# One written order for all engines from the last recurrence block to the entry of the feed-forward part

## The chip, the cores and the metric

The kernel runs on one core of a Trainium2 chip. A core has five engines, each with its own queue of instructions that it works through in order: TensorE (PE, matmuls, with PEld for its weight loads), VectorE (DVE), ScalarE (ACT), GpSimd (POOL) and SyncE (SP, which here issues nearly all DMA transfers). An instruction that waits for data holds everything behind it on its own engine. The metric is the time of one execution in device microseconds, as the median of the timed runs.

## What is computed

One hybrid decoder layer over 2048 tokens of width 1024, all in float32. Cut to what matters:

```python
xn   = rms_norm(h, pre_mix_norm)
proj = xn @ w_in                                   # state-space and recurrence inputs
y_ssd  = ssd_mixer(proj[:, :1544], ...)            # 8 heads, chunks of 128 tokens, gated by silu(z), normed
y_rwkv = rwkv7_mixer(proj[:, 1544:], ...)          # 8 heads: S = S*w + (S a) b + v k, y = S r, per token
mix = concat([y_ssd, y_rwkv]) @ w_out
h   = h + rms_norm(mix, post_mix_norm)
hn  = rms_norm(h, pre_ffn_norm)
u   = causal_dwconv(hn @ ffn_w_up, ...)            # 2 x 2816 columns, 3 taps
f   = (silu(gate(u)) * val(u)) @ ffn_w_down
out = h + rms_norm(f, post_ffn_norm)
```

## The kernel before

Matmul operands are split into a high and a low fp16 part, and each product is made of three matmuls (high x high, high x low, low x high). The work has three phases.

*R* (`phase_R`) is the recurrence: 16 blocks of 128 tokens. A block makes its input products (`d`, `c`), the gram matrices (`gr`), and a triangular solve on 32x32 pieces (`solve`: 31 small steps of L754 and L760 on POOL and DVE, then a round trip through DRAM, L766 and L772, and the products `pw` and `po`, L841 and L845). The second half of a block runs beside the first half of the next.

*S* (`phase_S`) is the state-space part: 8 pairs of two chunks of 128 tokens. Per chunk it makes the gate products `z` (L1216, a PSUM bank of its own with one buffer, emptied by ACT's copy `sz`, L1222), the decay products `bc` (L1261, L1262), the outputs `py` and `pf`, the state `pst`, and then the output projection `o` (L1344, 24 matmuls of 512 columns per half) with the post norm (L1347 to L1376). Per pair the cumulative decay is turned over on PE (`acs`, L1192: the flip), split into three bf16 parts on DVE (`pp`, L1195 to L1198), written to DRAM by SP (`rows`, L1200) and read back in another layout (`R`, L1255), one R per chunk. The post norm writes H (L1360), turns the normed tokens over by transposing transfers (`tu`, L1372, L1373), joins the parts on POOL (`hT`, L1375) and writes HN (L1376), which the feed-forward part reads. Output weights are loaded by SP as `ost` (L1116) and split by ACT and others (`split_w`, L287) into `wo`. The row roots of the norms are two short POOL instructions (L302, L303).

*F* (`phase_F`) is the feed-forward part in two halves of 1024 tokens, 22 column groups f in each, with seven products (L1658) per f over sums and differences of quarter blocks. Its operands are the token parts `b` (loads `hs`, splits at L1504) and the weight parts `w` (loads `us`, sums at L1630, splits at L1499 on ACT and L1506 on DVE). Products go through `C` (L1672 on ACT, L1676 on DVE), the convolution taps (L1711) and the gate, and every fourth f the `down` products (L1894) follow.

What sets the order: PE's instructions stand in the order in which the program writes them, everywhere. Block 15 of R is written by the plan `LAST`, the rest of it beside the first state-space steps by `DRAIN` and `S_DRAIN`, the state space by `S_PLAN` and `S_TAIL` (with steps of the first two f's of F in the places marked F). DVE, ACT, POOL and SP follow a written order only in the blocks up to 14 and in what `Program.run()` plans of F (from its third f on); between, the framework's scheduler orders their instructions by its own costs and the dependencies. Some of SP's loads are tied to an earlier transfer there by `pace` (L291), which adds an ordering with no semaphore. In F, `Program.add` (L69) plans a step when `prog.on` is set, and before that runs it at once:

```python
    def add(self, engine, us, fn, reads=(), writes=()):
        if not self.on:
            fn()
            return
```

## Time and profile before

| | |
|---|---|
| median of 3 timed runs | 2552.05 us (2547.22 to 2556.14) |
| the profiled execution | 2552.89 us |
| its span, first to last instruction | 2551.1 us |
| mean granted TensorE clock | 0.980 of full speed |
| PE busy | 2406.4 us, 94% of the span |
| DVE busy | 1921.5 us, 75% |
| last block of R alone on PE | about 814 to 864 us |
| end of R beside the first state-space chunks | about 864 to 932 us |
| output projection `o` | 937 to 1314 us |
| products of F | 1273 us to the end (1273.0 is the first, in between the last `o`) |
| products of f = 4 | about 1388 to 1405 us |

The profile is of one execution. A row of the timeline or of a group names its start and length in us, the engine, the line, the operation, the tile it writes and those it reads, the shape and, with x, how many instructions of one kind stand together; a bracket behind it is the idle time of the engine just before it and what ended it. A row of the waits names the engine and line that waited, the engine and line that it waited for, and the total in us, the number of waits and the longest. SPq is SP's queue of DMA issues; there a length is the time of issuing.

### The profile page before, as it was taken

How to read it: one execution, taken by the hardware profiler on the slowest of the kernel's cores; microseconds unless marked ns; L12 is line 12 of the kernel's file. 1: busy time of each engine (PE TensorE's matmuls, PEld its weight loads, DVE VectorE, ACT ScalarE, POOL GpSimd, SP SyncE). 2: the span in 40 equal slices, each digit the busy share in tenths (PEclk: the TensorE clock that was granted, in tenths of full speed). 3: DMA queues.
4: the chain of work that ended last, by engine and by line, in shares of the span. 5: the costliest groups of instructions: out<-in, count | busy, mean ns of one | idle time of the engine just before them, and what ended most of it. 6: DMA issues, size and time to landing. Idle time of an engine off the chain costs nothing. (4 is left out here: it accounts for less than half of the span.)

```text
span 2551.1 us, 53834 instructions
## 1 busy us (share of the span) xinstructions
PE 2406.4 (94%) x21212; PEld 1520.3 (60%) x21212; DVE 1921.5 (75%) x3687; ACT 1204.6 (47%) x2407; POOL 1231.3 (48%) x1237
## 2 busy tenths in 40 slices
PE   4899999999999899999988999999979999999998
PEld 4789999999998655555533444444434444444443
DVE  6768877877787557768888799999999826455557
ACT  6555666566556444445444554444543432213132
POOL 2233444344444524446687675686847622223135
PEclk8899999999999989999999999999999999999999
DMA  7233233323322445556664544544446543333243
GB/s 220 68 71 71 56 79 78 65 58 78 85 56 61 163 128 140 145 160 179 179 201 154 181 138 161 174 143 167 140 132 223 170 121 103 101 102 104 84 160 107
DMA packets 344412, 319.12 MB, mean 125 GB/s; under 512 B 203232, under 2 KB 248672, under 8 KB 340832
## 3 DMA queue, kind: packets, MB, share of 16 engines
q1 hardware_dynamic: 342864, 314.12, 41.8%
q8 instruction: 166, 2.72, 0.5%
q10 hardware_dynamic: 1296, 1.58, 0.2%
q14 instruction: 86, 0.70, 0.1%
HBM read 187.85 MB, written 110.99 MB: 117 GB/s over the span
## 5 line engine op out<-in xcount | busy, mean ns | idle before, releaser
L1658 PE MATMUL u<-b,w 128*128 128x512 f16 x3696 | 810.1, 381 | 29.7 <-DVE C L1676 10.2
L1658 PEld LDWEIGHTS <-w 128*128 128x128 f16 x3696 | 363.0, 98 | 473.9 <-issue 37.9
L324 PE MATMUL d<-xt,wr 128*128 128x129 f16 x5376 | 333.1, 224 | 25.1 <-DMA xt<-xh 15.6
L324 PEld LDWEIGHTS <-wr 128*128 128x128 f16 x5376 | 319.0, 100 | 40.2 <-issue 21.7
L1894 PE MATMUL d<-dw,fa 128*128 128x512 f16 x1512 | 332.0, 379 | 4.7 <-DMA dw<-DW 2.4
L1894 PEld LDWEIGHTS <-fa 128*128 128x128 f16 x1596 | 156.5, 98 | 204.5 <-issue 17.0
L1676 DVE TENSOR_TENSOR C<-u,C 128x512 f32<-128x512 f32 x220 | 150.5, 685 | 156.3 <-PE u L1658 146.4
L324 PE MATMUL c<-xt,wc 128*128 128x131 f16 x3072 | 198.8, 225 | 12.0 <-ACT rc L558 6.3
L324 PEld LDWEIGHTS <-wc 128*128 128x128 f16 x3072 | 184.2, 99 | 18.9 <-issue 11.0
L1907 DVE TENSOR_TENSOR acc<-d,acc 128x512 f32<-128x512 f32 x212 | 140.2, 683 | 52.7 <-PE d L1894 51.8
L1504 POOL TENSOR_TENSOR fa<-p,fa 128x512 f16<-128x512 f32 x100 | 142.3, 1436 | 40.3 <-ACT fa L1499 40.3
L1506 DVE SCALAR_TENSOR_TENSOR w<-us,w 128x512 f16<-128x512 f32 x132 | 146.0, 1117 | 14.8 <-ACT w L1499 13.7
L1711 DVE SCALAR_TENSOR_TENSOR p<-C,fpar,p 128x1024 f32<-128x1024 f32 x88 | 128.8, 1464 | 35.4 <-ACT p L1707 35.2
L582 DVE SCALAR_TENSOR_TENSOR ca<-c,cw,ca 128x128 f32<-128x128 f32 x360 | 113.5, 344 | 25.3 <-ACT ca L572 21.4
L754 DVE TENSOR_TENSOR tmp<-atl,xl 128x60 f32<-128x60 f32 (+24 forms) x465 | 119.1, 256 | 17.4 <-DMA atl<-ATd 5.9
L1711 DVE SCALAR_TENSOR_TENSOR a<-C,fpar,a 128x1024 f32<-128x1024 f32 x88 | 125.8, 1429 | 4.4 <-ACT a L1707 3.0
L1499 ACT ACTIVATE fa<-p 128x512 f16<-128x512 f32 x110 | 65.5, 623 | 132.6 <-DVE p L1724 120.8
L1630 POOL TENSOR_TENSOR us<-us,us 128x512 f32<-128x512 f32 x66 | 106.3, 1614 | 41.4 <-DVE w L1506 22.2
L760 DVE TENSOR_TENSOR xl<-xl,tmp 128x60 f32<-128x60 f32 (+24 forms) x465 | 113.0, 243 | 14.4
L1672 ACT ACTIVATE C<-u 128x512 f32<-128x512 f32 x88 | 52.2, 593 | 145.0 <-PE u L1658 128.0
L1717 POOL COPY fcarry<-C 128x2 f32<-128x2 f32 x88 | 41.1, 468 | 163.3 <-DVE C L1676 163.3
L1499 ACT ACTIVATE w<-us 128x512 f16<-128x512 f32 x132 | 80.6, 624 | 79.1 <-POOL us L1630 44.6
(325 smaller groups left out, 4425.5 us busy)
## 6 DMA issues: line engine op xcount, KB each, us to landing
UW<-w SPq DMA_DIRECT2D x154, 256.0 KB
w<-UW SPq DMA_DIRECT2D x154, 256.0 KB
us<-in_w_u_dram SPq DMA_DIRECT2D x88, 256.0 KB
DW<-dw SPq DMA_DIRECT2D x70, 256.0 KB
dw<-DW SPq DMA_DIRECT2D x56, 256.0 KB
hs<-HN SPq DMA_DIRECT2D x48, 256.0 KB
r<-in_w_d_dram SPq DMA_DIRECT2D x10, 1024.0 KB
xin<-in_x_dram SPq DMA_DIRECT2D x16, 512.0 KB
```

The lines of the kernel that those rows point to most:

```text
L324: nc.tensor.matmul(ps, w[:, a, kt, :], xt[:, b, kt, cols], start=n == 0, stop=n == 3 * KT - 1)
L582: V.scalar_tensor_tensor(out=acc[:, q], in0=m["rc", e][:, q, k:k + 128], scalar=cw[:, e + q, k:k + 1], in1=acc[:, q], op0=ALU.mult, op1=AL ...
L754: chain.tensor_tensor(out=self.tmp[:, :k, :n], in0=self.atl[:, j, j + 1:32].unsqueeze(1).to_broadcast([P, k, n]), in1=self.xl[:, :k, j:j + ...
L760: chain.tensor_tensor(out=self.xl[:, :k, j + 1:32], in0=self.xl[:, :k, j + 1:32], in1=self.tmp[:, :k, :n], op=ALU.add)
L1499: S.activation(h, src, AF.Copy, **({} if scale is None else {"scale": scale}))
L1504: {"V": V, "G": G_}[engine].tensor_tensor(out=l, in0=src, in1=h, op=ALU.subtract)
L1506: V.scalar_tensor_tensor(out=l, in0=src, scalar=scale, in1=h, op0=ALU.mult, op1=ALU.subtract)
L1658: nc.tensor.matmul(bk[at], self.w[i][:, u, k, :], self.half.b[i][:, k, v, :], start=start and n == 0, stop=n == 11, skip_group_check=True)
L1676: op("V", .61, lambda: V.tensor_tensor(out=part(j, x), in0=bk[at], in1=part(*a), op=ALU.add), (("u", 4 * s + at), (*(c0, c1)[a[0]], a[1])) ...
L1711: V.scalar_tensor_tensor(out=o[j], in0=C[j][:, 2 - d:1026 - d], scalar=cw[:, g, 2 - d:3 - d], in1=o[j], op0=ALU.mult, op1=ALU.add)
L1894: nc.tensor.matmul(bk[s, t], pairs[m].a[i][:, u, t * P:t * P + P], pairs[m].w[n][0][:, v, :], start=new and m == 0 and u == v == 0, stop=m ...
L1907: V.tensor_tensor(out=acc[j][:, t], in0=bk[s, t], in1=acc[j][:, t], op=ALU.add)
```

## The change

The phases are cut into named steps. A method such as `Chunk.y` or `Pair.flip` now returns a list of small functions, each for one to a few instructions, and the class `Steps` calls them by name, as R's blocks did already. A step's instructions are noted while they are traced. There are two tables: `TAIL` is the order in which the steps are traced, which sets PE's memory allocation and the dependencies; `ORDER` is one order of the same steps for all five engines, from the last steps of block 13 to the 460th step of F. For each step of `ORDER`, each of its instructions is put behind the previous one of its engine by an ordering that has no semaphore ("written order"). The 460 E steps are F's set-up (8), the steps of its first two f's, and the first 140 steps (`OPENED`) of what `Program.run()` planned for the rest. From there on `HANDS`, the planned order of before, goes on unchanged.

Besides: `pace` is gone, since the table says where SP's loads stand. Eight parameter loads (cst_s, dtb, Ab, Db, sdt, gpost, gpre2 and fpar) are issued by SP, where ACT issued them. F's products made before the planner is on are four steps of three matmuls each (one per k) instead of one step of twelve. The PSUM bank of `pf`, `py` and `pY` is chosen by the chunk's parity. The instructions themselves are as before: 34368 on PE, 3689 on DVE and 1242 on POOL in both programs; ACT goes from 2306 to 2298 and SP from 1284 to 1292, which is the eight loads. The order of PE, DVE, ACT, POOL and SP is the same in both programs up to the last block of R (the first difference on PE stands at 814 us of the profiled execution) and from f = 4 of F on (1388 to 1405 us).

Three places show how the order differs. The first is the drain, on ACT. Tiles ending in _14 or _15 belong to R's blocks, sz_1 and th_1 to state-space chunk 1, wo is the output weight. Before:

```order
L986 ACTIVATE yln_14_16994<-yt_14_16989,par_194 128x128 x4
L287 ACTIVATE wo_17701<-ost0_17710,sng_16792 128x1024
L287 ACTIVATE wo_17701<-ost1_17714,sng_16792 128x1024
L1222 ACTIVATE sz_1_17023<-z_1_16980 128x512
L992 ACTIVATE yo_14_17001<-yln_14_16994 128x4x128
L1223 ACTIVATE th_1_17024<-sz_1_17023 128x512
```

The same place on ACT now:

```order
L1456 ACTIVATE wo_17702<-ost0_17711,sng_17020 128x1024
L876 ACTIVATE ct_15_6_16902<-ca_15_6_16893 128x256
L1456 ACTIVATE wo_17702<-ost1_17715,sng_17020 128x1024
L1633 ACTIVATE sz_1_17257<-z_1_17214 128x512
L1274 ACTIVATE yln_14_17228<-yt_14_17223,par_194 128x128 x4
L1543 ACTIVATE de_1_17315<-de_1_17315 128x16
L1174 ACTIVATE qs_150_17175<-pq_150_17154 64x512
L1637 ACTIVATE th_1_17259<-sz_1_17257 128x512
```

The two splits of wo have another ACT step between them and sz_1 follows them, with the affine of block 14 (yln) behind it. The loads that the splits need stand on SP. XTd and XT1 are block 15's solve on its way through DRAM. Before:

```order
L766 DMA XTd_15_16302<-xl_15_16237 256x1x32 x4
L772 DMA XT1_230<-XTd_15_16302 32x8x32 x4
L1116 DMA ost0_17710<-in_w_o_dram 128x1024
L1116 DMA ost1_17714<-in_w_o_dram 128x1024
L1200 DMA rows_0_16978<-pp_0_16972 16x384
L1255 DMA R_0_16987<-rows_0_16978 3x8x128
L1255 DMA R_1_17278<-rows_0_16978 3x8x128
```

SP at this place now:

```order
L1434 DMA ost0_17711<-in_w_o_dram 128x1024
L1489 DMA xbc_1_17074<-XC1_66 128x2048
L1434 DMA ost1_17715<-in_w_o_dram 128x1024
L1054 DMA XTd_15_16538<-xl_15_16473 256x1x32 x4
L1434 DMA ost2_17719<-in_w_o_dram 128x1024
L883 DMA XC7_72<-ca_15_4_16818 128x2x128
L1060 DMA XT1_230<-XTd_15_16538 32x8x32 x2
L1584 DMA rows_0_17212<-pp_0_17206 16x384
```

The output weight loads stand ahead of XTd_15 instead of behind XT1, and xbc_1 and a convolution output (XC7) have moved between. The second place is on SP in the state space, at pair 2 (rows_2, R_4, R_5) beside the post norm of chunk 1 (tu_10 and tu_11, its two halves). Before:

```order
L1372 DMA_TRANSPOSE tu_10_18318<-hl_1_18300 128x4x128
L1373 DMA_TRANSPOSE tu_10_18318<-xi_1_17999 128x4x128
L1140 DMA xbc_3_18395<-XC3_68 128x2048
L1376 DMA HN0_81<-hT_10_18321 128x4x128
L1372 DMA_TRANSPOSE tu_11_18326<-hl_1_18300 128x4x128
L1373 DMA_TRANSPOSE tu_11_18326<-xi_1_17999 128x4x128
L1200 DMA rows_2_18360<-pp_2_18354 16x384
L1333 DMA yr_3_18472<-YR1_74 128x8x128
L1335 DMA xi_2_18260<-in_x_dram 128x1024
L1255 DMA R_4_18362<-rows_2_18360 3x8x128
L1255 DMA R_5_18622<-rows_2_18360 3x8x128
```

SP at this place now:

```order
L1878 DMA H1_84<-m_1_18027 128x1024
L1867 DMA_TRANSPOSE tu_10_18319<-xi_1_18000 128x4x128
L1584 DMA rows_2_18361<-pp_2_18355 16x384
L1686 DMA R_4_18363<-rows_2_18361 3x8x128
L1819 DMA yr_3_18473<-YR1_74 128x8x128
L1867 DMA_TRANSPOSE tu_11_18327<-xi_1_18000 128x4x128
L1867 DMA_TRANSPOSE tu_11_18327<-hl_1_18301 128x4x128
L1822 DMA xi_2_18261<-in_x_dram 128x1024
L1489 DMA xbc_3_18396<-XC3_68 128x2048
L1887 DMA HN0_81<-hT_10_18322 128x4x128
L1887 DMA HN0_81<-hT_11_18330 128x4x128
L1686 DMA R_5_18623<-rows_2_18361 3x8x128
```

rows_2 and R_4 stand ahead of the second half's transposes, and R_5 stands behind both HN writes of chunk 1. The third place is on DVE at the end of the state space, chunk 14's output yt_14 beside the first weight parts of F. Before:

```order
L1296 TENSOR_TENSOR yt_14_20776<-py_14_20917,yt_14_20776 128x512
L1297 TENSOR_TENSOR yt_14_20776<-yt_14_20776,sz_14_20830 128x512
L1305 TENSOR_SCALAR yt_14_20776<-yt_14_20776,sgr_20933 128x256 x2
L1317 TENSOR_TENSOR ST1_16803<-pst_14_20954,ST1_16803 128x512
L1235 TENSOR_TENSOR Xdt_15_20971<-px_15_20975,dtt_7_20462 128x512
L1239 TENSOR_TENSOR yt_15_20981<-px_15_20975,Db_16788 128x512
```

DVE at this place now:

```order
L1779 TENSOR_TENSOR yt_14_20774<-py_14_20918,yt_14_20774 128x512
L1796 TENSOR_TENSOR ST1_17026<-pst_14_20955,ST1_17026 128x512
L1780 TENSOR_TENSOR yt_14_20774<-yt_14_20774,sz_14_20831 128x512
L1654 TENSOR_TENSOR Xdt_15_20977<-px_15_20972,dtt_7_20479 128x512
L1978 SCALAR_TENSOR_TENSOR w4_0_0_21524<-us_0_001_21502,w4_0_0_21524 128x512
L1742 TENSOR_TENSOR of_15_20994<-pf_15_20991,E_7_20669 128x512
L1660 TENSOR_TENSOR yt_15_20979<-px_15_20972,Db_17019 128x512
L1976 TENSOR_TENSOR b2_0_21429<-hs00010_21416,b2_0_21429 128x512
L1978 SCALAR_TENSOR_TENSOR w1_0_0_21512<-us_0_000_21498,w1_0_0_21512 128x512
L1768 TENSOR_SCALAR yt_14_20774<-yt_14_20774,sgr_20935 128x256
```

The scaling by sgr stood right behind the product with sz; now the state, the next chunk's first steps and token and weight parts of F stand between.

The diff, cut to its core (a line or two of each table):

```diff
+class Steps:
+    made, kind = None, ""
+    def do(self, name, *a, only=None):
+        key = (name, *a)
+        if key not in self.todo:
+            self.todo[key] = getattr(self, name)(*a)
+        steps = self.todo[key]
+        for i in range(len(steps)) if only is None else (only,):
+            step, steps[i] = steps[i], None
+            if step:
+                note(".".join(str(v) for v in (f"{self.kind}{self.number()}", *key)) + f"/{i}", step)
...
-S_PLAN = """
-c.begin Z c.off c.decay.0 Z p.norm Z Z c.decay.1 p.o.0.0 p.o.0.1 c.keys t.sums q.post.0 s.steps q.post.1 c.y t.flip
-n.rows p.o.1.0 c.state p.o.1.1
-"""
...
+TAIL = """
+R14.solve R13.state.1 R13.finish.0 R14.d.13 R14.conv.7 R14.transposed.0 R13.values R14.conv.5 R15.load
...
+OPENED = 140
+ORDER = """
+R14.conv.7/9 R13.state.1/3 R15.d.0/0 R13.state.1/4 R14.conv.7/10 R13.state.1/6 R13.finish.0/0 R14.d.13/1 R15.d.1/0
...
-        def load_x(self):
-            self.xt = wk.tile([P, 2, KT, TB], F16, name="xs" + self.sf, tag="xt", bufs=2)
-            pace(tc, K, nc.sync.dma_start(self.xt, XN[self.b]), "atl")
+        def load(self, what):
+            def rows():
+                if what == 0:
+                    self.xt = wk.tile([P, 2, KT, TB], F16, name="xs" + self.sf, tag="xt", bufs=2)
+                    nc.sync.dma_start(self.xt, XN[self.b])
...
-        S.dma_start(fp, K.par_dram[:, NCOLS - NP_F:NCOLS])
+            early, mid, lambda: nc.sync.dma_start(K.fp, K.par_dram[:, NCOLS - NP_F:NCOLS]),
...
-                    def make():
+                    def make(some=range(4)):
...
+                    if not prog.on:
+                        for k in range(4):
+                            op("T", .65, lambda k=k: make((k,)))
+                        return
...
-        with tc.manual_schedule(engines={getattr(mybir.EngineType, x) for x in ("DVE", "Activation", "Pool", "SP")}):
-            prog.run()
+        todo = prog.run()
+        yield prog.entry + todo[:OPENED]
+        prog.on = None
+        with tc.manual_schedule(engines=HANDS):
+            for step in todo[OPENED:]:
+                step()
...
+    def behind(ins):
+        if ins.engine in last:
+            tc.add_manual_dep(ins, last[ins.engine].name, dep, reason="written order")
+        last[ins.engine] = ins
+
+    for step in ORDER.split():
+        for ins in made.get(step, ()):
+            behind(ins)
```

More of the change, by code (lines that the diff above doesn't have):

```diff
@@ new lines @@
+R15.merge.1 R15.update.0 C0.keys R15.state.0 C3.z.1 R15.own.1 C1.rows C0.y R15.update.1 C3.z.2 R15.state.1 R15.gate
+R15.finish.0 C0.state C3.z.3 R15.finish.1 rend E.0 X.right X.wo.0 X.wo.1 X.wo.2 X.wo.3 X.wo.4 X.wo.5 X.wo.6 X.wo.7
+P2.load.0 C1.begin C4.z.0 C1.off C1.decay.0 C4.z.1 C0.norm C4.z.2 C1.decay.1 C0.load.0 C0.load.1 C0.o.0.0 C0.o.0.1
+C1.keys P1.sums C1.y P1.flip C2.rows C0.o.1.0 C1.state C0.o.1.1 P2.load.1 C2.begin C4.z.3 C2.off C2.decay.0 C5.z.0
+C1.norm C5.z.1 C2.decay.1 C1.load.0 C1.load.1 C1.o.0.0 C1.o.0.1 C2.keys C0.post.0 P2.steps C0.post.1 C2.y C3.rows
@@ L256 @@
+E.378 E.424 C15.post.1/5 E.391 E.431 E.450 E.456 E.459 E.441 E.453 E.452 E.420 E.428 E.440 E.417 E.442 E.439 E.437
+E.446 E.458 E.457 E.448 E.449
 """
+HANDS = {getattr(mybir.EngineType, x) for x in ("DVE", "Activation", "Pool", "SP")}
 def load_consts(tc, K, pool, cst, par, rows, rows16):
@@ L1259, in decay @@
             hs, c, q = slice(4 * g, 4 * g + 4), self.c, self.q
-            bc = bank(f"bc{self.cf}{g}", "bc")
-            nc.tensor.matmul(bc, identb, mnegb, start=True, stop=False)
-            nc.tensor.matmul(bc, ones3, self.R[:, hs], start=False, stop=True)
-            for h in range(4):
-                S.activation(self.Dt[:, 4 * g + h], bc[:, h], AF.Exp, bias=q.nac[:, c, 4 * g + h:4 * g + h + 1])
-            V.tensor_tensor(
-                out=self.Dt[:, hs], in0=self.psc[:, g, :].unsqueeze(1).to_broadcast([P, 4, P]), in1=self.Dt[:, hs],
-                op=ALU.mult)
@@ L1268, in decay, with products @@
-            V.tensor_tensor(out=self.dec[:, hs], in0=bc[:, :, P - 1], in1=q.nac[:, c, hs], op=ALU.add)
-            S.activation(self.aend[:, hs], bc[:, :, P - 1], AF.Exp)
-            if g == 1:
-                S.activation(self.dec, self.dec, AF.Exp)
+            m = {}
+            def products():
+                m["bc"] = bank(f"bc{self.cf}{g}", "bc")
+                nc.tensor.matmul(m["bc"], X.identb, X.mnegb, start=True, stop=False)
+                nc.tensor.matmul(m["bc"], X.ones3, self.R[:, hs], start=False, stop=True)
@@ new lines, in y, with rows, products, square @@
+        def y(self):
+            def rows():
+                return self.yt.rearrange("p h s -> p (h s)")
+            def products():
+                py = self.py = bank_y("py" + self.cf, self.n).rearrange("p a b -> p (a b)")
+                for h in range(8):
+                    nc.tensor.matmul(
+                        py[:, 64 * h:64 * h + 64], self.Dt[:, h, :], self.Xdt[:, h, :], start=True, stop=True)
+            def square(g):
+                if g == 0:
+                    self.gs = wk.tile([P, 2], F32, name="sgs" + self.cf, tag="sgs")
+                    self.jk = wk.tile([P, 1024], BF16, name="sq" + self.cf, tag="sq")
@@ L2107, in hybrid_layer @@
-        next(F)
-        for _ in S:
-            next(F)
+        cp = ExitStack()
+        const = cp.enter_context(tc.tile_pool(name="const", bufs=1, side="left"))
+        tables = [io[n] for n in ("cst", "par", "rows", "rows16")]
+        K.hand = ExitStack()
+        blocks, front, rest = phase_R(
+            tc, K, const, tables, io["x"], io["w_r"], io["w_c"], io["wl"], io["g2"], XN, XC, YR)
+        pairs, chunks, setup = phase_S(tc, K, io["x"], io["w_z"], io["w_dt"], io["w_o"], XN, XC, YR, Hd, HN)
@@ new lines, in hybrid_layer @@
+        F = phase_F(tc, K, io["w_u"], io["w_d"], Hd, HN, out)
+        entry = next(F)
+        K.hand.close()
+    last = {ins.engine: ins for ins in traced(tc)}
+    Steps.made = {"tc": tc}
+    for step in TAIL.split():
+        step, _, part = step.partition("/")
+        name, *a = step.split(".")
+        if name == "front":
+            front()
+        elif name == "rend":
+            rest.close()
+        elif name == "const":
+            cp.close()
+        elif name == "E":
+            note(step, entry[int(a[0])])
+        elif name == "X":
+            setup.do(a[0], *(int(v) for v in a[1:]), only=int(part) if part else None)
+        else:
+            some = {"R": blocks, "P": pairs, "C": chunks}[name[0]]
+            some[int(name[1:])].do(a[0], *(int(v) for v in a[1:]), only=int(part) if part else None)
@@ L2111, in hybrid_layer @@
             pass
+    first = {}
+    for ins in traced(tc)[n:]:
+        if first.setdefault(ins.engine, ins) is ins:
+            behind(ins)
 def host_layout(inputs):
```

1082 lines of the change are left out of this document (701 added, 381 removed).

## The prediction

> **What bounds the kernel now.** I read the page first: the busy rows, then the span in 40 slices, to see whether one engine sets the time and where it doesn't.
>
> ```profile
> PE 2406.4 (94%) x21212; PEld 1520.3 (60%) x21212; DVE 1921.5 (75%) x3687; ACT 1204.6 (47%) x2407; POOL 1231.3 (48%) x1237
> PE   4899999999999899999988999999979999999998
> PEclk8899999999999989999999999999999999999999
> ```
>
> TensorE (PE) is busy 94% of the span. Each slice is 64 us. PE's digit drops below 9 at the start, at 829 to 893 us (the 14th slice), at 1276 to 1403 us, at 1850 to 1913 us and at the end; the clock's drops at 893 to 957 us. Elsewhere PE is the bound, and no order of the other engines can help there. The change leaves every order alone up to block 15 of the recurrence and from the fifth feed-forward step (f = 4) on, which the trace puts at 814 and 1405 us. So I cut the trace there, and inside by phase: the last block, its drain beside the first state-space chunks, the state-space phase, and its end with the entry of the feed-forward part.
>
> ```profile
> core 0: us, PE busy (x) PEld busy (x) DVE busy (x) ACT busy (x) POOL busy (x), PEclk, DMA share, GB/s
> 814.00:864.00 50.00, 44.95 (x745) 41.28 (x743) 31.56 (x79) 26.98 (x61) 29.18 (x50) 1.00 0.48 162
> 864.00:932.00 68.00, 54.23 (x477) 34.46 (x475) 39.76 (x98) 32.15 (x66) 26.73 (x48) 0.85 0.43 133
> 932.00:1200.00 268.00, 253.78 (x1492) 144.02 (x1490) 193.44 (x364) 121.12 (x337) 128.66 (x134) 1.00 0.53 147
> 1200.00:1405.00 205.00, 179.37 (x814) 84.42 (x815) 168.77 (x186) 98.52 (x193) 149.32 (x129) 0.93 0.58 178
> ```
>
> Length less PE busy is PE's idle time: 5.0, 13.8, 14.2 and 25.6 us, 58.6 us in all. Besides, the granted clock was 0.85 in the second stretch and 0.93 in the fourth, a loss of up to 0.15 x 68 = 10.2 and 0.07 x 205 = 14.4 us, part of it inside the gaps. Gaps and clock together are all that a new order can win, some 70 to 80 us; the matmuls stay. The waits say who holds PE (total, times, longest):
>
> ```profile
> PE bc L1262 <- DMA R<-rows: 8.7, 5, 2.4
> PE z L1216 <- ACT sz L1222: 8.4, 4, 7.7
> PE u L1658 <- DVE C L1676: 6.7, 2, 4.5
> PE u L1658 <- DVE b L1504: 6.2, 2, 4.6
> PE u L1658 <- ACT w L1499: 4.3, 1, 4.3
> PE bc L1261 <- ACT aend L1269: 3.6, 3, 2.0
> ```
>
> Six rows hold 37.9 of the 58.6 us: a DMA chain in the state-space phase, one long stall in the drain, and DVE and ACT in the entry of the feed-forward part.
>
> **The change, part by part.** It removes and adds nothing on PE; 8 parameter loads go from ACT's queue to SP's; the rest is order. I take the four stretches in turn.
>
> *814 to 864, last block.* PE's 5.0 us there are many short waits on links of chains that the new order spaces out. No row of before shows the new spacing: between nothing and all 5.0, I take half, 2.5.
>
> *864 to 932, drain.* These rows are ACT, PE, SP and the wait of SP ahead of them:
>
> ```profile
> 877.74 1.51 ACT L986 ACTIVATE yln<-yt,par 128x128 f32<-128x128 f32 x4 [1.33 <-PE yt L983]
> 887.20 2.42 ACT L287 ACTIVATE wo<-ost,sng 128x1024 f16<-128x1024 f32 x2 [7.96 <-DMA ost<-in_w_o_dram]
> 889.53 0.58 ACT L1222 ACTIVATE sz<-z 128x512 f32<-128x512 f32 x1
> 890.16 2.72 PE L1216 MATMUL z<-ws,xs 128*128 128x512 f16 x6 [7.70 <-ACT sz L1222]
> 883.48 0.92 SPq L1116 DMA_DIRECT2D ost<-in_w_o_dram  x2
> SPq L766 <- DVE xl L760: 20.9, 1, 20.9
> ```
>
> The z bank has one buffer, so PE's next z waits for ACT's sz copy (0.58 us). ACT works in order, and ahead of sz stand two splits of the output weights, whose loads SP issued only at 883.48, because it stood 20.9 us on the write of block 15's triangular solve. In the new order two of these loads are issued ahead of that write, so ACT finds its data there: the 7.7 us go. What is late next is the solve itself:
>
> ```profile
> L825 DVE STREAM_TRANSPOSE XW<-XT x2: 425/430/436, 883.3 to 884.5; 32x256 f32<-32x256 f32 x2
> L841 PE MATMUL pw<-XW,G x32: 191/191/212, 900.0 to 900.5; 32*32 32x32 f32 x32
> ```
>
> XW is ready at 884.9 and PE got to it at 900.0, a cover of 15 us, of which the 7.7 us take half. That leaves 7 us for the other gaps before it, so I don't take all of the remaining 6.1 us but half, 3. Of the clock loss of 10.2 us, which begins in this stall, I take 6. Together 7.7 + 3 + 6 = 17 us. If the solve's chain comes 8 us later in the new order, only 7 are won; with every gap and the full clock it would be 24. I stay above the middle, since the cover is a row of the trace and only its use is guessed.
>
> *932 to 1200, state space.* One of the five waits on R, with its chain:
>
> ```profile
> 989.10 0.28 PE L1192 MATMUL acs<-ident_s,nac 128*16 128x128 f32 x1
> 991.04 1.23 DVE L1198 TENSOR_TENSOR pp<-rr,pp 16x128 bf16<-16x128 f32 x1
> 994.38 1.21 SPq L1373 DMA_TRANSPOSE tu<-xi  x1
> 995.71 0.50 SPq L1200 DMA_DIRECT2D rows<-pp  x1
> 997.61 0.62 SPq L1255 DMA_DIRECT2D R<-rows  x2
> 1001.07 0.37 PE L1262 MATMUL bc<-R,ones 3*128 3x512 bf16 x1 [2.39 <-DMA R<-rows]
> ```
>
> From the flip's end (989.38) to R in place (1001.07) it takes 11.7 us. In it the rows' write is issued 3.4 us after pp is complete (992.27 to 995.71), because SP first issues two transposing transfers of the post norm. The new order puts the rows ahead of the second half's transposes, and R right behind. Without the 3.4 us the chain takes 8.3. PE's own work between flip and R was 11.7 - 2.4 = 9.3 us; in the new order it is about 7 us in this pair (24 o, 2 pb, 8 py and one bc, by the durations below) and 8 to 17 in the others. So this pair still waits some 1.1 us, others less. I leave 3.0 of the 8.7 us, the rest of 5.7 goes. Of the other 14.2 - 8.7 = 5.5 us, all short links, I take 2.3, in all 8. Bounds: 14.2 if all goes, and -6 if the rows or R come as late again as they now are early (7 pairs x 0.9 us of it uncovered).
>
> The short waits have a second cost, which these rows show:
>
> ```profile
> 1258.32 0.38 PE L1261 MATMUL bc<-mnegb,identb 128*128 128x512 bf16 x1 [1.96 <-ACT aend L1269]
> 1258.94 4.45 PE L1344 MATMUL o<-wo,yr 128*128 128x512 f16 x12
> 1263.23 2.75 PE L1344 MATMUL o<-wo,Y 128*128 128x512 f16 x12
> 1265.82 0.38 PE L1249 MATMUL pb<-ident_s,xbc 128*128 128x128 f32 x2
> 1266.04 1.23 PE L1294 MATMUL py<-Xdt,Dt 128*128 128x64 f32 x10
> ```
>
> Right behind a wait of 1.96 us twelve o products take 4.45 us, where the next twelve take 2.75: 1.7 us of clock lost to a short gap. I count these only inside the clock terms. The Trainium skill (TensorE: Matmul & The Clock Gate, Part 1) has the clock halve after an idle window of about 3.4 us or more. By that rule only the waits of 7.7, 4.6, 4.5 and 4.3 us would cost clock, and some 2 us of my sum would fall away; the trace differs, with its 1.96 us.
>
> *1200 to 1405, end of state space and entry of the feed-forward part.* PE waits for DVE and ACT here, and DVE is busy 168.8 of 205 us. What DVE itself waited for in this stretch:
>
> ```profile
> DVE w L1506 <- ACT w L1499: 7.9, 5, 2.9
> DVE xi L1364 <- POOL pnr L303: 7.3, 5, 2.7
> DVE m L1358 <- POOL por L303: 4.2, 4, 2.1
> DVE yt L1305 <- POOL sgr L303: 4.2, 3, 2.1
> ```
>
> DVE's 36.2 us of idle time are what the end of this stretch can come forward by. In the new order the scaling of yt has six other instructions between itself and its operand's last step instead of none, so sgr's 4.2 us go; the post norm's two waits (11.5) and ACT's splits (7.9) are spaced out less, and I take half, 9.7. That makes 13.9. Against it stands 2 us for DVE work that is stretched when POOL's share rises: the weight splits here take 674 ns at best and 1044 ns in the middle,
>
> ```profile
> L1506 DVE SCALAR_TENSOR_TENSOR w<-us,w x132: 674/1044/2840, 1241.0 to 1859.4; 128x512 f16<-128x512 f32 x132
> ```
>
> so 31 of them at 60 to 70 ns more are 2 us. That gives 12. Bounds: -5 (the gain taken back whole by stretched work and a worse wait) and 36. I stay nearer to the low end because DVE's order in this part hardly moves: the first token split stands 15 places earlier and the first weight split 6, in a stretch of 186 DVE instructions. Splitting F's first products into four pieces adds no matmul and lets PE start on pieces while DVE makes the next operand; it can gain nothing beyond DVE's own end.
>
> *The 8 loads on SP* cost about 0.5 us of issue each, as SP's rows of 0.50 and 0.62 us show, 4 us in all. They stand ahead of phases that use them tens of microseconds later, so I count nothing; uncovered, they cost those 4 us.
>
> **Sum.** 2.5 + 17 + 8 + 12 = 39.5 us against the profiled execution's 2552.9 us (span 2551.1; the median of the timed runs is 2552.05, so no shift is needed): 2513 us. About 0.3%, 7.7 us, is what a measurement of this kernel can tell from no change.
>
> **The rivals.**
>
> *B, DVE holds the entry.* A DVE instruction with two operands in SBUF is stretched beside POOL (1044 against 674 ns above), and a denser order puts more of POOL's 149.3 us beside DVE. If each of the 31 splits and as many other such instructions of this stretch take 0.2 us more, 12 us are gone, the fourth term is 0 and the time is 2525 us. For it: DVE at 168.8 of 205 us is the highest of the four stretches. Against it: DVE's idle waits are for short POOL chains, not for data. Chance 0.17. The Trainium skill (SBUF — State Buffer, Who interferes with whom) says that a DVE instruction with two SBUF inputs and a GpSimd instruction that reads SBUF exclude each other for a whole instruction; the spread of the splits fits this.
>
> *C, nearly all of it.* Three quarters of the 58.6 us idle, 44, and 16 of the 24.6 us of clock: 60 us, 2493 us. For it: PE shows 9 in eleven slices on end before 829 us, where the recurrence has stood in such an order already. Against it: the fourth stretch is short of DVE. Chance 0.08.
>
> *D, the change does not do what it says:* the chains (solve, R, post norm) set the pace, and each early start is handed back at the next link. Gain under 7.7 us, about 2550 us. Against it: the 7.7 us stall is one of order alone. Chance 0.06.
>
> *E, SP's queue.* All of SP's transfers now stand in one fixed row, and a transfer that isn't ready holds all behind it. SP stands on such waits already:
>
> ```profile
> SPq L1360 <- POOL m L1359: 60.7, 13, 5.9
> ```
>
> That is 4.7 us for each store of H. In the new order R of each odd chunk stands behind two HN writes that wait for POOL, and the feed-forward part's first token loads stand ahead of HN writes. If this makes R or the rows 7 us late in each of 7 pairs, with 0 of PE's work to cover it, PE loses 49 us, gaining 39.5 elsewhere: 2562 us. It decides from 6.7 us per pair. Against it: the odd chunk's R is used a whole chunk later. Chance 0.11.
>
> **How the numbers follow.** My forecast keeps 0.58. With B and C it is faster by over 0.3%: 0.83; D is the same, 0.06; E is slower, 0.11. The range reaches from a little below C (the drain's and entry's upper bounds) to D's near edge: 2486 to 2547 us, which leaves out E, part of D and what lies beyond C; the sum of all lower bounds (2557) and of all upper ones (2474) would need four misses on one side.
>
> **What would show it.** Right: no z wait over 1 us at the drain; the R waits at about 3 us in all; clock 1.00 where it was 0.85; XW to pw with no cover left; f = 4 reached some 40 us earlier, 12 of them after 1200 us on the old scale, with DVE idle near 22 us. Wrong: PE waits on XW or the solve of over 7 us (second term), R waits over 6 us (third), weight splits with a median over 1.2 us (rival B), or PE waits on R, yr or hs behind SP waits that are new (rival E). After f = 4 nothing should differ by more than 2 us.

## The result

| | kernel before | changed kernel |
|---|---|---|
| median of the timed runs | 2550.74 us (2547.22 to 2556.14, 4 runs) | 2530.72 us (2526.95 to 2533.15, 4 runs) |
| ratio, 95% interval | | 0.9918 [0.9896, 0.9941] |
| span of the profiled execution | 2551.1 us | 2530.1 us |
| mean granted clock | 0.980 | 0.983 |

The change makes the kernel 20 us faster, 0.8%. The forecast was 39.5 us: right direction, inside the range, half of the gain. A second set of runs of the changed kernel gave 0.9929 [0.9913, 0.9946].

The first two parts of the changed kernel's page:

```profile
PE 2397.2 (95%) x21207; PEld 1516.7 (60%) x21212; DVE 1893.3 (75%) x3687; ACT 1198.0 (47%) x2407; POOL 1219.6 (48%) x1237
PE   4899999999999999998878999999989999999998
PEclk8899999999999999999999999999999999999999
```

A slice is 63 us. The dent of the drain (the 14th slice of PE's row, the 15th of the clock's) is gone from both. The dent of the entry has grown: four slices, 1138 to 1391 us, down to 7, where it was two slices of 8. To see what each stretch is worth, I cut the new trace where PE has done as many matmuls as at 814, 864, 932, 1200 and 1405 us before:

```profile
808.80:855.40 46.60, 46.02 (x747) 42.30 (x745) 31.39 (x85) 27.90 (x62) 28.95 (x57) 1.00 0.46 143
855.40:903.00 47.60, 44.84 (x466) 28.80 (x466) 36.48 (x93) 30.75 (x70) 21.24 (x40) 1.00 0.58 182
903.00:1165.80 262.80, 255.82 (x1494) 145.84 (x1496) 171.82 (x354) 115.36 (x324) 120.49 (x131) 0.99 0.58 156
1165.80:1384.00 218.20, 178.38 (x815) 85.19 (x815) 168.06 (x201) 99.72 (x202) 153.75 (x133) 0.92 0.56 169
```

Against 50, 68, 268 and 205 us before, the stretches win 3.4, 20.4 and 5.2 us, and the last one **loses 13.2**. Another 5.2 us were won before the first cut: 2.1 of them between 804 and 814 us (801 to 809 now) and 3.1 ahead of that, nearly all between 113 and 175 us. There the program is as it was and the profiled execution of before shows a clock of 0.97 where the new one shows 1.00. The other traces with the new order show this lead too, except that of e7, so I don't count these 3 us to the change, and what they come from isn't shown.

PE was 34 us ahead when it had done the work of 1200 us, and 21 at f = 4. Behind f = 4 both executions take 1146.1 us, as the prediction expected. So the question for the experiments is where 13 us went, and whether the entry was worth the 12 us that the prediction gave it.

**The drain.** PE, then DVE, at the point where PE had stood 7.70 us on sz:

```profile
874.63 2.75 PE L1624 MATMUL z<-ws,xs 128*128 128x512 f16 x12
877.32 1.06 PE L1129 MATMUL pw<-XW,G 32*32 32x32 f32 x32
```

```profile
876.74 0.90 DVE L1113 STREAM_TRANSPOSE XW<-XT 32x256 f32<-32x256 f32 x2 [0.61 <-DMA XT<-XTd]
```

Twelve z products now run through without a stop and PE goes straight on to the solve's product at 877.32, on the first half of XW, whose second half is finished at 877.64. The cover of 15 us is used up to the last, and the solve costs PE nothing. Among PE's waits between 850 and 1205 us there is none of z:

```profile
PE pst L1789 <- DVE Xd L1718: 3.3, 1, 3.3
PE pst L1789 <- ACT Btok L1679: 2.6, 1, 2.6
PE acs L1570 <- DVE nac L1560: 2.5, 4, 1.3
PE bc L1697 <- ACT aend L1714: 1.9, 2, 1.4
PE o L1839 <- ACT m L1845: 1.8, 1, 1.8
...
PE bc L1698 <- DMA R<-rows: 0.6, 1, 0.6
```

R fell from 8.7 us in five waits to 0.6 in one.

**The entry.** What DVE waited for there (1165 to 1384 us), the counterpart of the four rows in the prediction:

```profile
DVE w L1978 <- ACT w L1971: 12.6, 8, 2.9
DVE b L1976 <- ACT b L1971: 5.5, 5, 2.3
DVE m L1875 <- POOL por L1612: 5.0, 4, 3.0
DVE a L2182 <- ACT a L2178: 4.7, 3, 3.5
DVE yt L1779 <- POOL yt L1746: 4.1, 1, 4.1
DVE yt L1768 <- POOL sgr L1612: 3.4, 1, 3.4
...
DVE xi L1880 <- POOL pnr L1612: 1.4, 2, 0.7
```

pnr's 7.3 us are nearly gone, sgr and por are much as they were, and ACT's splits make DVE wait 18.1 us (w and b), where the same two rows of before had 7.9 and 2.4. DVE's work is the same, 168.1 against 168.8 us, but its idle time rose from 36.2 to 50.1 us (218.2 less 168.1), where the prediction expected 22: as much as the stretch grew. Behind ACT stands a transfer. ACT's own waits from 1165 us on, in the changed kernel:

```profile
ACT w L1971 <- DMA UW<-w: 17.7, 3, 7.1
ACT w L1971 <- issue: 10.6, 3, 5.5
...
ACT m L1845 <- DMA H<-m: 9.8, 2, 6.3
ACT b L1971 <- DMA hs<-HN: 8.5, 3, 3.4
ACT w L1971 <- DMA us<-in_w_u_dram: 8.1, 3, 3.2
```

Four rows with DMA, 44.1 us. In the kernel before (1200 to 1405 us) the list begins so, with POOL at its head:

```profile
ACT w L1499 <- POOL us L1630: 15.7, 8, 3.4
ACT b L1499 <- DMA hs<-HN: 10.8, 4, 6.9
```

ACT waits now for the *stores* of w and H, whose buffers it wants to fill again. PE's longest wait of the entry, 9.49 us where none was over 4.6 before, ends such a chain (UW is the DRAM copy of w):

```profile
1334.57 0.63 ACT L1971 ACTIVATE w<-us 128x512 f16<-128x512 f32 x1 [7.02 <-DMA UW<-w]
1335.26 20.72 PE L2125 MATMUL u<-b,w 128*128 128x512 f16 x84 [9.49 <-ACT w L1971]
```

SP's queue shows, on a store of H, how a store can come late. POOL finished chunk 11's m at 1180.35:

```profile
1178.00 2.35 POOL L1877 TENSOR_TENSOR m<-m,xi 128x1024 f32<-128x1024 f32 x1 [1.69 <-DVE m L1875]
```

```profile
1186.52 1.19 SPq L1867 DMA_TRANSPOSE tu<-xi  x1
1195.79 0.33 SPq L2012 DMA_DIRECT2D hs<-HN  x1
1196.16 0.55 SPq L1819 DMA_DIRECT2D yr<-YR  x1
1196.81 0.60 SPq L1878 DMA_DIRECT2D H<-m  x1
```

```profile
1201.33 0.60 ACT L1845 ACTIVATE m<-o 128x512 f32<-128x512 f32 x1 [6.28 <-DMA H<-m]
```

SP issued nothing from 1187.7 to 1195.79. Its waits between 1186 and 1197 us say why:

```profile
SPq L2012 <- DVE b L1976: 8.1, 1, 8.1
```

The token load hs waits for a buffer that a token split on DVE (b) has still to read. H, ready at 1180.35, went out 16 us later, and ACT stood 6.28 us on it. (e11 below takes away this wait and not the stores' of w.)

### The profile page after: what moved, and what is told of

The parts are those of the page before. It is cut to its first block, busy times and chain, and to the rows that moved or that the text cites. A ratio compares the mean times of both kernels' runs of the same rounds, so it can differ in the third digit from the quotient of the medians.

```text
span 2530.1 us, 53854 instructions
## 1 busy us (share of the span) xinstructions
PE 2397.2 (95%) x21207; PEld 1516.7 (60%) x21212; DVE 1893.3 (75%) x3687; ACT 1198.0 (47%) x2407; POOL 1219.6 (48%) x1237
## 5 line engine op out<-in xcount | busy, mean ns | idle before, releaser
L618 PE MATMUL d<-xt,wr 128*128 128x129 f16 x5376 | 333.8, 224 | 19.6 <-DMA xt<-xh 14.6
L1978 DVE SCALAR_TENSOR_TENSOR w<-us,w 128x512 f16<-128x512 f32 x132 | 141.0, 1079 | 19.6 <-ACT w L1971 18.5
```

The source lines that it names most:

```text
L618: nc.tensor.matmul(ps, w[:, a, kt, :], xt[:, b, kt, cols], start=n == 0, stop=n == 3 * KT - 1)
L1978: V.scalar_tensor_tensor(out=l, in0=src, scalar=scale, in1=h, op0=ALU.mult, op1=ALU.subtract)
```

## The experiments

Theory A: the chains and stalls of the first three stretches were paid by order alone and are gone for good; the entry is bound by DVE's work and its short links, so PE's 13 us were lead of PE alone and could not be kept. Theory B: the entry lost them to one part of the new order, SP's single row above all, and the lead is there to be had. "Lead" in an expectation is how much earlier a point is reached than in the kernel before. Times are medians; the kernel before, measured beside them, took 2554.89 us (e1, e2, e4, e5), 2555.78 (c0, e6, e7, e9), 2553.72 (e8, e10, e11) and 2553.54 (e12). Ratios are to those; the changed kernel's are 0.9918 and 0.9929. A span is that of one execution, and the times of the changed kernel's four executions lie 6 to 7 us apart in each set, so small differences of spans say little.

| label | time, us | ratio, 95% interval | span, us |
|---|---|---|---|
| c0_after_again | 2535.80 | 0.9929 [0.9913, 0.9946] | 2531.1 |
| e1_z0_twice | 2544.81 | 0.9958 [0.9944, 0.9973] | 2546.0 |
| e2_drain_loads | 2543.40 | 0.9955 [0.9939, 0.9971] | 2542.8 |
| e4_free_all | 2540.33 | 0.9944 [0.9927, 0.9962] | 2536.7 |
| e5_free_sp | 2526.64 | 0.9887 [0.9864, 0.9911] | 2526.6 |
| e6_old_entry | 2535.77 | 0.9923 [0.9908, 0.9938] | 2534.5 |
| e7_free_sp_all | 2543.81 | 0.9959 [0.9946, 0.9972] | 2548.4 |
| e8_rows_late | 2547.24 | 0.9972 [0.9958, 0.9986] | 2543.1 |
| e9_unsplit | 2533.37 | 0.9912 [0.9897, 0.9927] | 2532.7 |
| e10_sp_ready | 2529.76 | 0.9902 [0.9884, 0.9921] | 2527.6 |
| e11_sp_ready_s | 2532.05 | 0.9911 [0.9893, 0.9928] | 2527.2 |
| e12_w_twice | 2551.51 | 1.0 [0.9985, 1.0014] | 2549.7 |

### The changed kernel once more

> The changed kernel as it is, once more, so that the others of this call have it on the same chip: ratio to the kernel before 0.990 to 0.994, a median 14 to 25 us below it.

The same kernel, on the chip of e6, e7 and e9. Its ratio lies 0.0011 from the first one, well inside both intervals, and its entry shows the same rows (ACT waits 16.9 us on stores of w). The lost lead is no accident of one execution.

### Only the drain's loads put back (second term)

The four output weight loads go behind block 15's writes and reads on SP, with the splits that use them and sz_1 behind (here and below the tables are cut to the steps that move):

```diff
 R15.solve/77
 R15.values/4
+R15.solve/78 X.wo.0/0 X.wo.1/0 X.wo.0/1 X.wo.0/2 X.wo.1/1 C1.z.3/1 X.wo.1/2 X.wo.2/0 X.wo.2/1 X.wo.3/0
 R15.turn/0
```

> The changed kernel with one place of its order put back: SP issues the first output weight loads (ost0 to ost3) behind block 15's solve (XTd, XT1), and the splits of wo and the gate copy sz_1 wait for them on ACT, as before. Everything else follows the new order. The second term of the prediction valued this place at 17 us, 7.7 of them the wait of z for sz. Theory A (the entry swallows PE's lead): the stall is back in the trace, but the time rises by 6 us or less. Theory B (stretches add): it rises by 10 to 17 us, to 2541 to 2548.

The drain, between the same two points of PE's work, and PE's first wait in it:

```profile
854.00:915.90 61.90, 48.62 (x467) 29.65 (x466) 35.57 (x93) 30.84 (x70) 21.81 (x40) 0.89 0.45 140
```

```profile
PE z L1624 <- ACT sz L1633: 9.5, 1, 9.5
```

47.6 us became 61.9: the wait of 9.5 us is back, and the clock falls from 1.00 to 0.89. The place of four loads on one queue, with the splits and sz_1 that follow them on ACT, is worth 14.3 us in a stretch that won 20.4; 12.7 us of it arrive in the span (2542.8 against 2530.1), and 7 to 9 us in the times by the ratios. So most of the drain's lead isn't swallowed by the entry.

### More work for PE in the state space (is PE's lead only PE's?)

```diff
-                for k in range(2):
-                    for u, v in ((0, 0), (0, 1), (1, 0)):
+                for r in range(1 if g else 2):
+                    for k in range(2):
+                        for u, v in ((0, 0), (0, 1), (1, 0)):
```

> The changed kernel with the first six gate products (z.0) of each of the 16 state-space chunks made twice: 96 more matmuls of 512 columns at 229 ns (2.75 us for 12), 22 us of PE work more, spread over 855 to 1215 us, nothing else changed. The changed kernel's PE stood 34 us ahead of the kernel before at the point that the kernel before reached at 1200 us, and 20 us at f = 4. Theory A, the entry of the feed-forward part is paced by chains over DVE, ACT, POOL and SP that do not start earlier because PE does: most of the added work disappears in PE's waits there, and the time rises by 8 us or less, to 2539 at most. Theory B, the stretches add up and the entry is slower for a reason in its own order: the time rises by 20 to 23 us, to about 2552.

Between both theories: 16 us in the span, 7 to 10 in the times by the ratios. The lead of the post norm's first DVE step (m, L1875) over the kernel before tells more. In the changed kernel it is 33 us at chunk 0, 28 at chunk 11, 22 at chunk 12 and 21 at chunk 15; here 29, 16, 10 and 9. So the extra work of PE held DVE back inside the state space already, and the drop of 6 us between chunks 11 and 12 is the same in both. At f = 4 the leads are 21 and 6 us (its products end at 1383.7 and 1399.4, before at 1405.0). (All leads of DVE are from single traces.) The entry behind chunk 12 took little from either: what comes out is DVE's lead at chunk 12, 22 us, and not the 34 us that PE showed at 1200.

### The rows behind the transposes again (third term)

In pairs 2, 3, 5 and 6 the write of the rows goes behind the transposes that it had passed:

```diff
-C3.decay.1/8 P2.flip/2 C4.rows/0
+C3.decay.1/8
...
+C1.post.1/2 P2.flip/2 C4.rows/0
```

> The changed kernel with the write of the decay rows put behind the two transposes of the post norm's second half on SP, where the kernel before had it, in the pairs 2, 3, 5 and 6 (in 1, 4 and 7 the new order has nothing to put back); R follows. The prediction's third term gave 3.4 us to that place in the chain of each pair, with PE's own work covering part. By it the waits of PE for R rise from 0.6 to 4 to 9 us in all and the time by 3 to 8 us. If the new order's PE work between flip and R covers the chain anyway, the time stays within 2 us.

PE's waits from 850 to 1220 us begin with

```profile
PE bc L1699 <- DMA R<-rows: 9.2, 4, 3.8
```

The wait is back for four pairs (9.2 us against 0.6), and it costs 13 us in the span (2543.1) and 11 to 14 in the times, more than the wait. The state space, between the same two points of PE's work as 903.00 to 1165.80 in the changed kernel:

```profile
902.40:1178.80 276.40, 261.02 (x1498) 146.92 (x1497) 172.89 (x354) 115.25 (x325) 121.67 (x132) 0.98 0.54 150
```

PE's idle time rose from 7.0 to 15.4 us, and the matmuls took 261.0 us instead of 255.8, at a clock of 0.98 instead of 0.99. The third term's mechanism holds. 276.4 us is more than the 268 of the kernel before, so e8 is not the old order of this stretch, and its 13 us is what the place is worth inside the new order.

### The entry in the manner of before (fourth term)

From the 53rd F step on (about 1164 us) PE goes in the order of the program's text, and DVE, ACT, POOL and SP by the framework's scheduler, as before the change:

```diff
+FREE = {getattr(mybir.EngineType, x) for x in ("DVE", "Activation", "Pool", "SP")}
...
+        cut = cut or step == "E.53"
...
-            behind(ins)
+            if cut and ins.engine in FREE:
+                tc.add_manual_dep(ins, last[ins.engine].name, dep, reason="written order")
+                loose.append(ins)
+            elif cut and ins.engine == mybir.EngineType.PE:
+                rest.append(ins)
+            else:
+                behind(ins)
```

> The changed kernel with its written order cut for all engines from about 1164 us on: PE follows the order in which the steps are traced (the order of the kernel before), DVE, ACT, POOL and SP the scheduler's. Ahead of the cut everything is new. With SP alone set free the time fell, with DVE, ACT and POOL set free too, beside PE's new order, it rose. Theory D (the entry of before was the better one, and the new row of all five engines costs the 15 us): the lead of some 30 us is kept, 12 us or more below the changed kernel of this call. Theory C (SP's row alone is at fault, the rest of the new entry is better than the scheduler's): equal to the changed kernel within 6 us, or slower.

0.9923 against 0.9929 on the same chip: no difference. The written order of the entry, the only thing that this kernel takes away, is worth nothing as a whole. This is the failed term. (e5 shows that SP's part of it costs time, so the other engines' part would have to win about as much.)

### The entry with PE as now and the other four engines free, and with SP alone free

The edit is the same without the PE branch. FREE holds all four engines in e4, and in e5

```diff
+FREE = {getattr(mybir.EngineType, x) for x in ("SP",)}
```

> The changed kernel with the written order cut for DVE, ACT, POOL and SP from about 1164 us on (PE keeps its order): these four are ordered by the framework's scheduler up to f = 4, as in the kernel before. The entry took 220 us where it took 205 before. Theory A (chains of work pace the entry, whatever the order): within 6 us of the changed kernel. Theory C (the written order of the entry costs the 15 us): 2515 to 2522 us. If the written order is worth what the prediction said, it gets slower, by 10 us or more.

> The same cut for SP alone: DVE, ACT, POOL and PE keep the written order, SP's transfers from about 1164 us on stand in the scheduler's order. In the changed kernel's entry ACT waited 44 us for transfers (UW 17.7, H 9.8, hs 8.5, us 8.1), before it 13 us. Theory C, in the form that SP's row is the cause (rival E at another place): 8 to 14 us faster, 2517 to 2523. Theory A: within 4 us of 2530.7.

With all four free the span is 6.6 us longer, and PE waits 25.6 us on ACT's and DVE's C between 1166 and 1385 us, where it waited 11.0: this order of the four engines doesn't suit PE's. With SP alone free the kernel is the fastest of all, 0.9887. ACT's waits there (1165 to 1383 us):

```profile
ACT w L1972 <- issue: 14.0, 2, 7.6
...
ACT w L1972 <- DMA us<-in_w_u_dram: 7.6, 2, 4.4
ACT b L1972 <- DMA hs<-HN: 6.5, 5, 2.5
```

The stores of w, 17.7 us, are gone from the list. DVE's two waits on ACT's splits fall from 18.1 to 8.0 us, and PE's on ACT's w from 9.5 to 3.1; next in line is a wait of 5.7 us on DVE's w. f = 4 ends at 1380.8 instead of 1383.7 (1384.7 in c0), the span is 3.5 to 4.5 us shorter, and the time 8 to 11 us by the ratios. The end of f = 4 hides a part of it: this execution came to the entry 2 to 3 us later than the two of the changed kernel, with the same order up to there. From the z product that starts at 1165.81 in the changed kernel to the last product of f = 4, first there, then in e5:

```profile
1165.81:1383.32 217.51, 177.69 (x812) 84.86 (x812) 167.38 (x200) 99.14 (x201) 153.07 (x132) 0.92 0.56 168
1168.37:1380.42 212.05, 178.59 (x812) 85.64 (x811) 173.15 (x201) 100.09 (x202) 155.38 (x133) 0.93 0.59 175
```

That is 5.5 us (5.9 against c0, whose stretch is 217.9), and DVE's idle time in it falls from 50.1 to 38.9 us.

### SP free from the beginning of the table

As e5, with the cut at the table's first step:

```diff
+        cut = cut or step == "R14.conv.7/9"
```

> The changed kernel with SP set free over the whole length of the change, from block 13's last steps to f = 4; DVE, ACT, POOL and PE keep the written order. If SP's written row is at fault everywhere: 12 us or more below the changed kernel. If only in the entry, and in the drain and the state space it is what won the time (loads ahead of the solve, rows ahead of the transposes): the gain of the entry, some 6 us, is outweighed by a loss ahead of 1164 us, and the time is within 5 us of the changed kernel or above it.

2543.81 against 2535.80 on the same chip, 8 us slower. Between the same points of PE's work the drain takes 57.9 us (47.6 in the changed kernel), the state space 272.3 (262.8) and the entry from that z product 211.4 (217.5). Ahead of the entry SP's written row is worth time, and only in the entry does it cost, 6 us here as in e5.

### SP's row sorted by when its data is ready

SP's steps between 1105 and 1379 us (e10) or between 1105 and 1231 us (e11) are put in order of the time at which the changed kernel's trace has their data ready. 124 of 174 steps, or 31 of 77, change places; the other engines keep theirs.

```diff
-C11.y/0 E.38 C10.norm/0 C11.z.3/2 C11.load.0/0
+C11.y/0 C8.post.1/5 C10.norm/0 C11.z.3/2 E.38
```

> The changed kernel with SP's transfers between 1105 and 1379 us put into the order in which their data were ready in the changed kernel's profiled execution (124 of 174 change place; loads that did not wait keep their neighbour); all other engines keep the written order. In that execution the store of H of chunk 11 was issued 16 us after its data, behind a token load that waited for its buffer, and the stores of the first weight parts up to 45 us after theirs. Theory C (SP's written row is what hands the lead back): the lead of 28 us that the post norm of chunk 11 still has is kept to f = 4; 7 to 12 us below the changed kernel, a ratio to the kernel before of 0.987 to 0.990. If another engine's chain is next at the same length, within 3 us of the changed kernel, 0.991 to 0.994.

> The same for SP's transfers from 1105 to 1231 us only (31 of 77 change place: stores of H and HN and transposes of the state space ahead of token loads; the stores of weight parts stay late). If the 6 us lost between the post norms of chunks 11 and 12 come from the store of H behind the token load: the post norm of chunk 12 starts 4 to 6 us earlier, and 4 to 6 us of gain are left at the end (ratio 0.990 to 0.991). If the weight parts' stores are the costlier part: under 3 us.

Spans of 2527.6 and 2527.2 us, 2.5 and 2.9 below the changed kernel's; by the ratios 0.0016 to 0.0027 and 0.0007 to 0.0018 lower, which the intervals don't fully separate. ACT's waits on stores of w are gone in e10 as in e5, and from the same z product to the end of f = 4 it takes 214.8 us instead of 217.5. In e11 the wait on the store of H is gone and those on stores of w are not:

```profile
ACT w L1971 <- DMA UW<-w: 17.5, 3, 7.2
```

There this stretch takes 217.8 us, as in the changed kernel; its lower span was won ahead of it, most of it ahead of the first transfer that it moves. So the traces point to the stores of the weight parts as what costs, and the late store of H shown above cost little. But the lead of the post norms still falls from 28 us to 24 between chunks 11 and 12 in e10, and from 33 to 28 in e11. SP's row is a part of the loss, 3 us (e10) to 6 us (e5, e7) of this stretch, not all of it.

### The early products in one piece

The four steps of each early product stand together again; of one of them:

```diff
-E.94 E.154 C14.o.0.0/0 E.111
-E.155
...
-E.156
+E.94 C14.o.0.0/0 E.111
...
+E.128 E.154 E.155 E.156 E.157
```

> The changed kernel with the four pieces of each early product of the feed-forward part (f = 0 and 1) put together again on PE, at the place of the last piece; the other engines keep their order. If the pieces let PE work while DVE makes the next operand, PE loses up to 1.7 us per product where it waits now, some 5 us. If DVE and ACT set the pace there whatever PE does: within 3 us of the changed kernel.

0.9912 against 0.9929 [0.9913, 0.9946]: no difference that these runs can tell. Splitting them had gained nothing.

### More work for DVE in the entry

The low half of each weight part is written twice:

```diff
-                    V.scalar_tensor_tensor(out=l, in0=src, scalar=scale, in1=h, op0=ALU.mult, op1=ALU.subtract)
+                    for _ in range(1 if prog.on is None else 2):
+                        V.scalar_tensor_tensor(out=l, in0=src, scalar=scale, in1=h, op0=ALU.mult, op1=ALU.subtract)
```

> The low half of a weight part w is made twice by DVE for all weight parts of f = 0 to 3 and some of f = 4 (33 more DVE instructions in the entry, 941 to 994 ns each in the changed kernel's trace, so about 31 us of DVE work with nothing else changed; DVE was idle 50 us there). It tells what the entry is bound by. Theory A, DVE's own end sets the entry (as the prediction's fourth term assumed: idle time won on DVE is time won): nearly all of the 31 us shows, the time comes out 20 to 31 us above the changed kernel's 2531 to 2536, so 2552 to 2565. Theory B, the entry is set by single links (the first weight parts through ACT, SP's queue and the feed-forward part's first products) and DVE has room: 0 to 8 us above it, 2531 to 2543, and the extra work stands in DVE's idle time. A third outcome, 9 to 19 us, would say that DVE's idle is half room and half chain.

The entry to the same 813 matmuls of PE, first in the changed kernel, then here:

```profile
1165.80:1383.70 217.90, 178.08 (x813) 85.06 (x813) 167.76 (x200) 99.42 (x202) 153.45 (x133) 0.92 0.56 169
```

```profile
1165.80:1402.00 236.20, 185.93 (x813) 86.87 (x813) 195.47 (x234) 98.18 (x199) 150.97 (x132) 0.88 0.53 154
```

DVE's work grew by 27.7 us, its idle time shrank from 50.1 to 40.7, the stretch grew by 18.3, and the span by 19.6. Two thirds of the work added on DVE show in the time, and only a third fits into its 50 us of idle time. That is at the edge between theory A and the third outcome: DVE's work sets most of the entry's length, and its idle time, tied to links as the rows above show (ACT's splits, POOL's row roots), takes up only a third of more work. Theory B's "DVE has room" falls. One rival is left: the added work stands in the weight parts, for which PE's products wait, so a part of the 18.3 us can be the longer link itself. Work added to DVE off these links would tell; it wasn't tried.

## Why the prediction was right, and where it was wrong

**What bounds the kernel.** The sum of what the stretches won, 2.1 + 3.4 + 20.4 + 5.2 - 13.2 = 17.9 us, and the 3.1 us ahead of them are the 21.0 us of the span. Right for the first three stretches: the time came from PE's gaps and clock, at the places named.

**First term, 2.5 us.** 3.4 measured, and 2.1 more ahead of the cut. PE's idle time there fell from 5.0 to 0.6 us.

**Second term, 17 us.** 20.4 measured. The mechanism is shown by e2: loads behind the solve's write, z on sz, the clock. I had taken half of the gaps behind the 7.7 us; nearly all went (PE idle 13.8 to 2.8 us) and the clock is 1.00. The solve's chain was the bound that I feared, and it ended exactly when PE arrived.

**Third term, 8 us.** 5.2 measured on PE. The mechanism is right: R's waits are at 0.6 us, below the 3.0 that I left, and PE's idle time fell by 7.2 (14.2 to 7.0 us). The clock took 2 of that back (0.99 in 262.8 us, before 1.00). e8 puts the rows' place in four pairs at 11 to 14 us inside the new order, which is more than the whole stretch won and so no measure of this term.

**Fourth term, +12 us: this is the step that failed.** Measured, it is nothing (e6), and the stretch on PE is 13.2 us longer, beyond the lower bound of -5 that the prediction gave it. That the time still fell inside the range is owed to the width of the range. The prediction took DVE's 36.2 us of idle time as what could be won, and expected the new order to space out the waits on sgr, por, pnr and ACT's splits. pnr went (7.3 to 1.4). sgr's 4.2, which I counted as gone whole for six instructions in between, stayed at 3.4; por rose to 5.0. And the wait on ACT's splits, of which I took half as won, went from 7.9 to 12.6 us, since ACT now stood 17.7 us on stores of w in SP's row: with SP free (e5) these stand no more and the wait is 5.8. That DVE's time decides there was right for the most part (e12), and that 13.9 us of its idle time were to be had by this order was wrong. Even with SP free, 38.9 us of it are left, more than before.

It was also wrong to add the terms as if each us that PE wins ahead of the entry arrives at its end. PE had 34 us at 1200, DVE's post norm 28 at chunk 11 and 22 at chunk 12, and DVE's lead is what came out. The second and third terms still arrive for the most part, since their stalls were in DVE's way too (e2: 12.7 of 14.3 us).

**The loads on SP at nothing.** No row contradicts it. Not tried by itself. The prediction's sum of all lower bounds, 2557 us, leaves out the 4 us that it gave them uncovered; with them it is 2561.

**Rival B, DVE stretched beside POOL.** Its time (2525) came nearest to the result, and its mechanism didn't come about. The weight splits in the entry, changed kernel:

```profile
L1978 DVE SCALAR_TENSOR_TENSOR w<-us,w x31: 678/692/1758, 1214.8 to 1381.0; 128x512 f16<-128x512 f32 x31
```

The median is 692 ns, where the same 31 instructions had 964 before (941 and 1145 on average). Some others of the entry went the other way, the post norm's m from 1482 to 1857 ns, but DVE's work there is no larger, with 15 instructions more. In the state space too, DVE is stretched less, not more:

```profile
L1718 DVE TENSOR_TENSOR Xd<-Xdt,dec 128x512 f32<-128x512 f32 x16 | 13.0, 811 | 0.9 <-ACT dec L1727 0.9
L1641 DVE SCALAR_TENSOR_TENSOR sz<-th,sz 128x512 f32<-128x512 f32 x16 | 12.3, 771 | 0.0
```

```profile
L1273 DVE TENSOR_TENSOR Xd<-Xdt,dec 128x512 f32<-128x512 f32 x16 | 22.4, 1400 | 0.3 <-ACT dec L1271 0.3
L1224 DVE SCALAR_TENSOR_TENSOR sz<-th,sz 128x512 f32<-128x512 f32 x16 | 18.8, 1172 | 1.8 <-ACT th L1223 1.8
```

Over the whole kernel DVE's busy time fell by 28.2 us (1921.5 to 1893.3) with the same 3687 instructions. The rule that the prediction cites from the Trainium skill (SBUF — State Buffer, Who interferes with whom) fits these rows. Of the 16 Xd, 13 ran beside a POOL instruction before, in 1566 ns on average, and 7 do now, in 976; the others take about 680 in both kernels.

**Rival C** didn't come true: the entry was short of DVE, as its "against" said. **Rival D**, each early start handed back at the next link, is true of a part: 13 us of PE's lead. **Rival E**, SP's queue, named the right mechanism in the wrong place. R and the rows aren't late, and the odd chunk's R behind two HN writes shows no wait to speak of (0.6 us in all); but weight parts' stores that go out late cost 3 to 6 us in the entry by the traces (e5, e7, e10).

**What stays open.** By the traces, freeing SP gives back 5.5 to 6 of the 13 us; by the ratios of e5 it is 8 to 11, with intervals of 4 to 6 us on each side. The rest isn't traced to a link. The changed kernel and the variants that keep DVE's row lose 3 to 6 us of DVE's lead between the post norms of chunks 11 and 12, also where SP's row is in the order of ready data (e10), and why isn't known. DVE has 201 instructions left at the entry's start where it had 186, four more token splits among them, while it was idle for 91 of 262.8 us in the state space; at e12's rate, 0.66 us for each us of DVE work, pulling the token splits forward would by this estimate be worth a few us. That wasn't tried.

## What to carry to other kernels

A gain on the bounding engine arrived here only as far as the engine that bounds the next stretch came forward with it: measure the lead of that engine too, before adding up stalls. Idle time of an engine need not be room: lay extra work on it and see how much shows (here two thirds). One written row for all engines paid on the queue where places matter (the loads ahead of the solve, the rows ahead of the transposes), and cost on the same queue where stores that free a buffer went out late behind transfers that weren't ready; the best version here, e5 at 0.9887 [0.9864, 0.9911], keeps the written row and leaves SP free in the entry.

## What the hardware showed besides

Short waits cost clock here as well. PE in the changed kernel, behind a wait of 3.27 us:

```profile
1188.21 2.08 PE L1789 MATMUL pst<-Xd,Btok 128*128 128x256 f32 x4 [3.27 <-DVE Xd L1718]
1190.08 1.06 PE L1804 MATMUL pY<-ident_s,yt 128*128 128x128 f32 x4
1190.93 2.69 PE L1624 MATMUL z<-ws,xs 128*128 128x512 f16 x6
```

Six z products take 2.69 us, where twelve took 2.75 in the drain above: about half speed for some 5 us from the wait's end, with the rows between; the granted clock from 1188.2 to 1193.7 us is 0.53. Behind the 1.96 us of the prediction's row it was 0.50 from 1260 to 1262 us. The rule that the prediction cites from the Trainium skill (TensorE: Matmul & The Clock Gate, Part 1), an idle window of about 3.4 us or more, leaves this wait out by a little and the 1.96 us of before by far; the rows decide.
